# A blocked 8192 x 8192 transpose: four loads in two parts from two queues, no timing copies before a chunk, other places for the first stores

## The chip, the cores and the metric

The kernel runs on one core of a Trainium2 chip. The metric is the time of one execution on the device, in microseconds; lower is better. One more execution is taken with the profiler on, and every row below comes from that one.

## What is computed

```python
def setup_inputs():
    return {"x": np.random.randn(8192, 8192).astype(np.float32)}

def reference(x):
    return np.transpose(x)
```

The input has 268.4 MB and so has the output. Every element is read from HBM once and written once.

## The kernel before

**Tiles.** The input is cut into 128 chunks: chunk t holds 128 rows of x and 4096 columns, 2 MB. Chunks 0 to 63 cover the left half of the columns from top to bottom, 64 to 127 the right half. A chunk lies in SBUF with one row to a partition, 16 KB each. It is cut into 16 ranges of 256 columns. TensorE transposes a range as two 128 x 128 blocks (line 372, against the identity matrix `ident`), so a chunk takes 32 transposes, which fill two halves of PSUM: ranges 0 to 7 are evicted by ScalarE, 8 to 15 by VectorE (line 300, function `copies`).

**Stores.** A store collects up to 16 blocks of chunks that follow each other, so that long pieces go to HBM. Store w takes from chunk t the range with the index w modulo 16, for the 16 chunks t = w - 15 to w; the first fifteen stores are shorter, 1 to 15 cells, and after the last chunk fifteen shorter ones flush what is left. The range of chunk w that belongs to store w goes straight from PSUM to the store's region (the direct copy, "arena<-ps"); the ranges for later stores go to a buffer `slots` first, and the function `gather` (line 262, VectorE) moves what earlier chunks left there into the region, just before the direct copies of chunk w. In the program's order VectorE runs `gather(w)` and then `copies(w)`.

**Places in SBUF.** One buffer, `arena`, has 86 places of 1 KB in every partition. Three areas of 16 places hold loaded chunks; 38 further places are for the stores' regions (one of their areas holds an early chunk too, as four loads are under way at the start). A small planner (lines 114 to 153) walks over loads and stores in the order of their due times and gives each a place; `before` then names what has to have left that place: of a load, that its chunk is transposed, of a store, that it has landed. `gather` waits for these. From store 6 (`over`) on, a region starts at the lower or at the upper end of the 38 places, whichever comes free sooner, so from store 15 on two regions of 16 alternate.

**Order.** SP issues all transfers on one queue, in the order of the list `order`: store t - 1, then the load two to four chunks ahead of t. Before a store it waits for the direct copy (`closed`), before a load for the end of the transposes of the chunk in that area. Each transfer adds 16 to a semaphore, 1 for each of the 16 DMA engines that carry it.

**The start of a chunk.** For chunks 12 (`E`) to 125, TensorE waits for both halves of PSUM, runs two warming passes (line 366, `IDLE = 2`, 512 columns each, results overwritten), waits for `s_go`, then for the load's semaphore, and transposes. `s_go` comes from ScalarE: in the function `work`, it waits for the chunk's load and then runs `REST = 2` copies of the identity matrix into its half of PSUM, one after the other (line 405); what they write is overwritten by the transposes. They do nothing but take time. TensorE's part is a loop over three chunks (lines 387 to 391).

Of the kernel before, what the change touches and what calls it, by code (L numbers as in the profile page):

```python
# [40 lines left out]
def kernel(  # L41
# [5 lines left out]
    nc = tc.nc  # L47
    P = 128
    N, M = x.shape
    assert x.shape == out.shape[::-1]  # L50
    dt = x.dtype
# [10 lines left out]
    E = 12  # L62
# [48 lines left out]
    order += [("S", T - 1)] + [("S", w) for w in flush]  # L111


    due = {}
    sent = 0
    for k in order:
# [14 lines left out]
    for _, k, size, until in sorted(wanted):  # L131
        if k[0] == "L":
            o = spot(k[1])
        else:
            w = k[1]
            lo = NIN * NR if w < T - 2 else 0
            hi = END - NR if w < over else END
            late = lambda o: max([f for _, a, z, f in users if a < o + size and o < z], default=0)
            at = range(lo, hi - size + 1)
            if over <= w < T - 2:  # L140
                at = (lo, hi - size)
            elif w == T - 2:
                at = [spot(T - 3)]
            o = min(at, key=lambda o: (late(o), o))
        home[k] = o
        before[k] = sorted({u for u, a, z, _ in users if a < o + size and o < z}, key=lambda u: due[u])
        users = [
            (u, c, d, f)
            for u, a, z, f in users
            for c, d in ((a, min(z, o)), (max(a, o + size), z))  # L150
            if c < d
        ]
        users.append((k, o, o + size, until))

    with tc.tile_critical():  # L155
        ident = nc.alloc_sbuf_tensor("ident", [P, P], dt).ap()
        nc.alloc_sbuf_tensor("pad", [P, 64], dt)
        slots = nc.alloc_sbuf_tensor("slots", [P, (NR * (NR - 1) // 2) * PIECE], dt).ap()
        arena = nc.alloc_sbuf_tensor("arena", [P, END * PIECE], dt).ap()
        pss = [nc.alloc_psum_tensor(f"ps{k}", [P, J // 2], dt).ap() for k in range(2)]  # L160
# [5 lines left out]
        s_free = [nc.alloc_semaphore("s_fra"), nc.alloc_semaphore("s_frv")]  # L166
        s_cp = [nc.alloc_semaphore("s_cpa"), nc.alloc_semaphore("s_cpv")]
        s_g = nc.alloc_semaphore("s_g")
        s_go = nc.alloc_semaphore("s_go")
        s_rest = nc.alloc_semaphore("s_rest")  # L170
        s_x = [nc.alloc_semaphore("s_xa"), nc.alloc_semaphore("s_xv")]

        stored = [0] * (2 * W - 1)
# [4 lines left out]
        closed = {}  # L178
        shut = [0, 0]

        REST = 2
        LAST = T - 1 - (T - 1 - E) % NIN


# [11 lines left out]
        def free(eng, k):  # L198
            if k[0] == "L":
                eng.wait_ge(s_pe, 4 * k[1] + len(steps(k[1])))  # L200
            else:
                eng.wait_ge(s_st[lane(k[1])], done[k[1]])

        def load(t):
            s, c = divmod(t, CH)
            o = home["L", t] * PIECE
            for u in before["L", t]:
                free(nc.sync, u)
            nc.sync.dma_start(
                out=arena[:, o:o + J], in_=x[c * P:(c + 1) * P, s * J:(s + 1) * J]  # L210
            ).then_inc(s_ld[home["L", t]], 16)
# [126 lines left out]
        while order[first] == ("L", first) and not before[order[first]]:  # L338
# [11 lines left out]
            pattern=[[-1, P]],  # L350
            channel_multiplier=1,
        ).then_inc(s_id, 1)
        nc.scalar.sem_inc(s_free[0], 1)
        nc.vector.sem_inc(s_free[1], 1)

        def transposes(t):
            o = home["L", t]
            for g in range(NR):
                h, u = divmod(g, NR // 2)
                if u == 0 and not (h and E <= t < LAST):  # L360
                    nc.tensor.sem_inc(s_free[h], -1).wait_op(s_free[h], 1, "sem-ge")
                if g == 0:
                    if E <= t < LAST:
                        nc.tensor.sem_inc(s_free[1], -1).wait_op(s_free[1], 1, "sem-ge")  # L364
                        for _ in range(IDLE):
                            nc.tensor.matmul(out=pss[1][:, :4 * P], lhsT=ident, rhs=four, start=True, stop=True)  # L366
                    if E <= t < LAST:
                        nc.tensor.sem_inc(s_go, -1).wait_op(s_go, 1, "sem-ge")
                    nc.tensor.sem_inc(s_ld[o], -16).wait_op(s_ld[o], 16, "sem-ge")  # L369
                q = (o + range_at(t, g)) * PIECE  # L370
                for b in range(B):
                    tr = nc.tensor.transpose(  # L372
                        pss[h][:, (u * B + b) * P:(u * B + b + 1) * P],
                        arena[:, q + b:q + PIECE - B + b + 1:B],
                        ident,
                    )
                if g + 1 in steps(t):
                    tr.then_inc(s_pe, 1)
# [15 lines left out]
            transposes(t)  # L394

        worked = [0]
        rested = [0]

        def work(t):
            while worked[0] <= t:  # L400
                u = worked[0]
                if E <= u < LAST:
                    nc.scalar.wait_ge(s_ld[home["L", u]], 16)
                    for k in range(REST):
                        cp = nc.scalar.copy(  # L405
                            out=pss[0].rearrange("p (k i) -> p k i", i=P), in_=ap(ident, 0, [[0, J // 2 // P], [1, P]])
                        )
                        if k < REST - 1:
                            cp.then_inc(s_rest, 1)
                            rested[0] += 1  # L410
                            nc.scalar.wait_ge(s_rest, rested[0])
                    cp.then_inc(s_go, 1)
                gather(u, u)
                if u == T - 1:
                    gather(T, u)
                copies(u)
                worked[0] += 1
# [44 lines left out]
```

## Time and profile before

| What | Value |
|---|---|
| median of 3 runs | 1275.12 us |
| the runs | 1271.99, 1275.12, 1289.13 us |
| the profiled execution: its time | 1278.15 us |
| the profiled execution: its span | 1276.4 us |
| TensorE matmuls, share of the span | 66% |
| TensorE weight loads | 50% |
| VectorE | 48% |
| ScalarE | 54%, of it 426.3 us in 228 timing copies |
| DMA packets | 41334, 537.10 MB, mean 421 GB/s |

The span is what the profile covers; 1.75 us of the time lie outside it. PE is TensorE's matmuls, PEld its weight loads, DVE VectorE, ACT ScalarE, POOL GpSimd, SP the engine that issues the transfers; SPq or PEq is an engine's sequencer. "out<-in" names what is written and read; L28 is the line at which all stores but the first are issued, L209 that of the loads. "PEclk" is the granted TensorE clock, 1.00 being full speed, and "DMA share" the mean busy share of the 16 DMA engines; it can show a little over 1, as a packet is counted from before its predecessor's end. In a list of waits stand who waited and for whom, the total in us, how many times, and the longest. In a timeline stand the start, the length, and in brackets the idle time of the engine before it with what ended it.

### The profile page before, as it was taken

What the parts mean: (1) busy time and instruction counts of PE and PEld (TensorE: products, weight loads), DVE (VectorE), ACT (ScalarE), POOL (GpSimd) and SP (SyncE); (2) the same over time, 40 slices, a digit from 0 to 9 for tenths busy, and PEclk for the clock granted to TensorE, in tenths of its full rate; (3) what the DMA queues carried; (4) which work ended last, traced back from release to release, by engine and by line L of the source; (5) the groups of instructions that cost most, each with busy time, mean ns of one, the idle gap of its engine ahead of it and who ended that gap; (6) DMA issues with size and microseconds to landing.
All of it is one profiled execution on the core that took longest, in us unless ns stands there. A gap on an engine that the chain in (4) does not pass through costs nothing. (4 is left out here: it accounts for less than half of the span.)

```text
span 1276.4 us, 12056 instructions
## 1 busy us (share of the span) xinstructions
PE 837.0 (66%) x4552; PEld 642.4 (50%) x4552; DVE 615.1 (48%) x715; ACT 683.9 (54%) x630; POOL 0.7 (0%) x6
## 2 busy tenths in 40 slices
PE   6657866777676776666666666666666767666630
PEld 6655555544555555455545554554445545555530
DVE  3454454544554455445544544455445454455381
ACT  2235665566556556655665566555655556555510
POOL 0000000000000000000000000000000000000000
PEclk9877889988998889899898989999999898999865
DMA  9999999999999999999999999999999999999997
GB/s 394 412 413 361 412 428 430 428 432 430 432 430 432 430 432 430 432 430 432 429 428 430 429 429 430 431 431 432 431 431 432 430 399 420 426 428 419 407 396 327
DMA packets 41334, 537.10 MB, mean 421 GB/s; under 512 B 4576, under 2 KB 5216, under 8 KB 8288
## 3 DMA queue, kind: packets, MB, share of 16 engines
q1 hardware_dynamic: 41312, 536.89, 99.5%
q14 instruction: 18, 0.15, 0.0%
q8 instruction: 4, 0.07, 0.0%
HBM read 268.44 MB, written 268.44 MB: 421 GB/s over the span
## 5 line engine op out<-in xcount | busy, mean ns | idle before, releaser
L372 PEld LDWEIGHTS ps<-ident,arena 128*128 128x128 f32 x4096 | 553.6, 211 | 263.5 <-issue 263.5
L372 PE MATMUL ps<-ident,arena 128*128 128x128 f32 x4096 | 570.5, 303 | 156.7 <-PEq L369 156.2
L262 DVE COPY arena<-slots 128x2048 f32<-128x2048 f32 (+7 forms) x316 | 304.2, 1012 | 497.3 <-DMA out_dram<-arena 488.5
L405 ACT COPY ps<-ident 128x2048 f32<-128x2048 f32 x228 | 426.3, 1870 | 57.0 <-DMA arena<-in_x_dram 52.3
L366 PE MATMUL ps<-ident 128*128 128x512 f32 x456 | 270.4, 724 | 235.2 <-PEq L364 235.2
L300 ACT COPY slots<-ps 128x1024 f32<-128x1024 f32 (+2 forms) x335 | 238.5, 780 | 247.6 <-DVE arena L262 213.3
L300 DVE COPY slots<-ps 128x512 f32<-128x512 f32 (+2 forms) x336 | 289.4, 913 | 64.3 <-PE ps L372 62.8
L366 PEld LDWEIGHTS ps<-ident 128*128 128x128 f32 x456 | 88.8, 216 | 322.9 <-issue 322.9
L300 ACT COPY arena<-ps 128x256 f32<-128x256 f32 x66 | 24.5, 373 | 238.3 <-DVE arena L262 191.1
L300 DVE COPY arena<-ps 128x256 f32<-128x256 f32 x63 | 26.8, 425 | 77.4 <-PE ps L372 76.1
L300 ACT ACT_TABLE_LOAD x1 | 1.3, 1283 | 1.0 <-SPq L155 1.0
L344 POOL TENSOR_SCALAR_AFFINE_SELECT ident<-ident 128x128 f32<-128x128 f32 x1 | 0.3, 294 | 0.2 <-POOL ident L342 0.2
L342 POOL MEMSET ident<- 128x128 f32 x1 | 0.2, 205 | 0.5 <-SPq L155 0.5
L446 POOL MEMSET const-bfloat16-1.0<- 128x1 bf16 x1 | 0.1, 103 | 0.0
L446 POOL MEMSET const-uint8-127<- 128x1 uint8 x1 | 0.1, 103 | 0.0
L446 POOL MEMSET const-float32-0.0<- 128x1 f32 x1 | 0.1, 100 | 0.2 <-issue 0.2
L446 POOL MEMSET const-float32-1.0<- 128x1 f32 x1 | 0.1, 100 | 0.0
## 6 DMA issues: line engine op xcount, KB each, us to landing
arena<-in_x_dram SPq DMA_DIRECT2D x128, 2048.0 KB, 20.4
out_dram<-arena SPq DMA_DIRECT2D x98, 2048.0 KB, 16.6
out_dram<-arena SPq DMA_DIRECT2D x4, 1920.0 KB, 11.1
out_dram<-arena SPq DMA_DIRECT2D x4, 1792.0 KB, 11.1
out_dram<-arena SPq DMA_DIRECT2D x4, 1664.0 KB, 11.1
out_dram<-arena SPq DMA_DIRECT2D x4, 1536.0 KB, 10.8
out_dram<-arena SPq DMA_DIRECT2D x4, 1408.0 KB, 11.5
out_dram<-arena SPq DMA_DIRECT2D x4, 1280.0 KB, 12.4
```

Of the source, the lines that this page charges most:

```text
L262: cp = nc.vector.tensor_copy(out=ap(arena, do, [[P, len(v)], [dist, B], [1, P]]), in_=ap(slots, so, [[gap, len(v)], [P, B], [1, P]]),)
L300: cp = eng.copy(out=dst, in_=i) if e == 0 else eng.tensor_copy(out=dst, in_=i)
L342: nc.gpsimd.memset(ident, 0.0).then_inc(s_id, 1)
L344: nc.gpsimd.affine_select(out=ident, in_=ident, compare_op=mybir.AluOpType.not_equal, fill=1.0, base=0, pattern=[[-1, P]], channel_multipl ...
L366: nc.tensor.matmul(out=pss[1][:, :4 * P], lhsT=ident, rhs=four, start=True, stop=True)
L372: tr = nc.tensor.transpose(pss[h][:, (u * B + b) * P:(u * B + b + 1) * P], arena[:, q + b:q + PIECE - B + b + 1:B], ident,)
L405: cp = nc.scalar.copy(out=pss[0].rearrange("p (k i) -> p k i", i=P), in_=ap(ident, 0, [[0, J // 2 // P], [1, P]]))
L446: nc = _bacc.Bacc("TRN2", target_bir_lowering=False, num_devices=1)
```

## The change

**No timing copies.** `REST`, the copies of line 405 and the semaphores `s_go` and `s_rest` are gone. TensorE waits for the two halves of PSUM, runs the two warming passes, waits for the load and begins. ScalarE goes from the copies of one chunk straight to those of the next.

**Places of the first stores.** For stores 0 to 14 the list `young` names the place inside the 38, and the planner's choice is skipped. The places of stores 6 to 9 and 12 differ; all others keep theirs, but some of them follow other stores than before. So `gather` waits for other transfers:

| store | waited before for | waits now for |
|---|---|---|
| 7 | stores 0 to 3 | load 5 |
| 8 | load 5, store 6 | stores 0 to 3 |
| 9 | stores 3, 7 | stores 5, 6 |
| 10 | load 5, store 8 | load 5, stores 6, 7 |
| 11 | stores 4, 9 | stores 3, 4, 8 |
| 12 | load 5, store 10 | stores 4, 5, 9 |
| 14 | load 5, store 12 | stores 10, 12 |
| 15 | stores 4, 5, 13 | stores 12, 13 |
| 16 | load 5, store 14 | stores 12, 14 |

**Four loads in two parts.** Chunks 32, 60, 88 and 116 are loaded by `load_apart`: rows 0 to 119 by a DMA of GpSimd's, rows 120 to 127 by one of SP's at the place in SP's order where the whole load stood. Both queues wait first for the transposes of the chunk that was in the area. GpSimd waits for both landings and then adds 16 to the load's semaphore, for which TensorE waits as before. Ahead of the first of these loads, at the kernel's start, GpSimd copies 5 rows of 256 bytes into a spare buffer (`turn_engines(5)`), and ahead of each of the other three, right before it, 1 row (`turn_engines(1)`), and waits for that each time. The spare buffer has the size of the former `pad`. GpSimd's other work, making the identity matrix at the start, is as it was; otherwise it was idle.

```diff
+    young = [0, 1, 3, 6, 10, 15, 22, 29, 0, 17, 27, 0, 14, 0, 23]
...
-            if over <= w < T - 2:
+            if w < len(young):
+                at = [lo + young[w]]
+            elif w < T - 2:
                 at = (lo, hi - size)
...
-        nc.alloc_sbuf_tensor("pad", [P, 64], dt)
+        spare = nc.alloc_sbuf_tensor("spare", [P, 64], dt).ap()
...
-        REST = 2
...
+        APART = (32, 60, 88, 116)
+        PART = P - P // 16
+        gp = [0]
+
+        def turn_engines(n):
+            nc.gpsimd.dma_start(out=spare[:n, :], in_=x[:n, :64]).then_inc(s_gp, 16)
+            gp[0] += 16
+            nc.gpsimd.wait_ge(s_gp, gp[0])
+
+        def load_apart(t):
+            s, c = divmod(t, CH)
+            o = home["L", t] * PIECE
+            for u in before["L", t]:
+                free(nc.sync, u)
+                free(nc.gpsimd, u)
+            if t > APART[0]:
+                turn_engines(1)
+            nc.gpsimd.dma_start(
+                out=arena[:PART, o:o + J], in_=x[c * P:c * P + PART, s * J:(s + 1) * J]
+            ).then_inc(s_gp, 16)
+            nc.sync.dma_start(
+                out=arena[PART:, o:o + J], in_=x[c * P + PART:(c + 1) * P, s * J:(s + 1) * J]
+            ).then_inc(s_few, 16)
+            gp[0] += 16
+            nc.gpsimd.wait_ge(s_gp, gp[0])
+            nc.gpsimd.wait_ge(s_few, 16 * (APART.index(t) + 1))
+            nc.gpsimd.sem_inc(s_ld[home["L", t]], 16)
+
         def load(t):
             s, c = divmod(t, CH)
             o = home["L", t] * PIECE
+            if t in APART:
+                load_apart(t)
+                return
...
+        turn_engines(5)
...
-                    if E <= t < LAST:
-                        nc.tensor.sem_inc(s_go, -1).wait_op(s_go, 1, "sem-ge")
                     nc.tensor.sem_inc(s_ld[o], -16).wait_op(s_ld[o], 16, "sem-ge")
...
-                if E <= u < LAST:
-                    nc.scalar.wait_ge(s_ld[home["L", u]], 16)
-                    for k in range(REST):
-                        cp = nc.scalar.copy(
-                            out=pss[0].rearrange("p (k i) -> p k i", i=P), in_=ap(ident, 0, [[0, J // 2 // P], [1, P]])
-                        )
-                        if k < REST - 1:
-                            cp.then_inc(s_rest, 1)
-                            rested[0] += 1
-                            nc.scalar.wait_ge(s_rest, rested[0])
-                    cp.then_inc(s_go, 1)
                 gather(u, u)
```

More of the change, by code (lines that the diff above doesn't have):

```diff
@@ L168 @@
         s_g = nc.alloc_semaphore("s_g")
-        s_go = nc.alloc_semaphore("s_go")
-        s_rest = nc.alloc_semaphore("s_rest")
+        s_gp = nc.alloc_semaphore("s_gp")
+        s_few = nc.alloc_semaphore("s_few")
         s_x = [nc.alloc_semaphore("s_xa"), nc.alloc_semaphore("s_xv")]
@@ L396 @@
         worked = [0]
-        rested = [0]
         def work(t):
```

## The prediction

> **What bounds the kernel now.** I read the page first: what the DMA engines moved in each of 40 slices of the span, and how full the queues were.
>
> ```profile
> GB/s 394 412 413 361 412 428 430 428 432 430 432 430 432 430 432 430 432 430 432 429 428 430 429 429 430 431 431 432 431 431 432 430 399 420 426 428 419 407 396 327
> ...
> q1 hardware_dynamic: 41312, 536.89, 99.5%
> q14 instruction: 18, 0.15, 0.0%
> ```
>
> The packets of the data queue fill 99.5% of 16 DMA engines, at 430 to 432 GB/s through the middle: the kernel is bound by its transfers there. At 430 GB/s the 536.89 MB take 536,890 / 430 = 1248.6 us, so 27.8 us of the span of 1276.4 are lost somewhere. The busy time in ten stretches says where; it also shows TensorE busy for 546 of 800 us in the middle, and no other compute engine for more.
>
> ```profile
> core 0: us, PE busy (x) PEld busy (x) DVE busy (x) ACT busy (x) POOL busy (x), PEclk, DMA share, GB/s
> 0.00:20.00 20.00, 10.95 (x75) 10.82 (x76) 5.33 (x8) 5.42 (x8) 0.70 (x6) 1.00 0.92 377
> 20.00:100.00 80.00, 52.09 (x332) 48.68 (x331) 36.99 (x45) 24.78 (x35) 0.00 (x0) 0.81 1.01 415
> 100.00:130.00 30.00, 21.68 (x105) 16.10 (x104) 13.92 (x17) 16.51 (x14) 0.00 (x0) 0.81 0.90 355
> 130.00:200.00 70.00, 50.97 (x277) 37.85 (x276) 36.09 (x43) 43.40 (x43) 0.00 (x0) 0.90 1.00 421
> 200.00:1000.00 800.00, 546.04 (x2951) 411.18 (x2949) 392.30 (x454) 468.04 (x418) 0.00 (x0) 0.92 1.01 430
> 1000.00:1210.00 210.00, 142.38 (x738) 105.47 (x738) 99.58 (x114) 119.57 (x105) 0.00 (x0) 0.90 1.00 418
> 1210.00:1232.00 22.00, 12.94 (x85) 12.26 (x83) 15.92 (x20) 6.13 (x10) 0.00 (x0) 0.81 0.91 385
> 1232.00:1269.40 37.40, 0.00 (x0) 0.00 (x0) 14.99 (x19) 0.00 (x0) 0.00 (x0) 0.50 1.00 415
> 1269.40:1274.20 4.80, 0.00 (x0) 0.00 (x0) 0.00 (x0) 0.00 (x0) 0.00 (x0) 0.50 0.07 27
> 1274.20:1276.40 2.20, 0.00 (x0) 0.00 (x0) 0.00 (x0) 0.00 (x0) 0.00 (x0) 0.50 0.00 0
> ```
>
> A stretch loses its length times (1 - rate / 430): 2.5 us to 20, 2.8 to 100, 5.2 to 130, 1.5 to 200, nothing from there to 1000, 5.9 to 1210, 2.3 to 1232, 1.3 to 1269.4, 4.5 to 1274.2 and 2.2 to the end, together 28.2. Two kinds are to be told apart. Where the DMA share is about 1.01, the engines always had packets and these were slow (20 to 100, 130 to 200, 1000 to 1210). Where it is lower, engines had nothing to do: 100 to 130 (0.90), 1210 to 1232 (0.91) and the last row but one. There the share is 0.07, about one engine of 16 (0.0625), and the rate is 27 GB/s, a sixteenth of 430: for 4.8 us a single DMA engine works off what the other fifteen have long finished. It is that much behind.
>
> Next the waits, and a stretch of the timeline in the steady part.
>
> ```profile
> DVE arena L262 <- DMA out_dram<-arena: 488.5, 114, 11.5
> ```
> ```profile
> 1130.15 0.54 SPq L28 DMA_DIRECT2D out_dram<-arena  x1
> ...
> 1132.16 3.77 ACT L405 COPY ps<-ident 128x2048 f32<-128x2048 f32 x2 [0.35 <-DMA arena<-in_x_dram]
> ...
> 1132.38 1.95 PE L366 MATMUL ps<-ident 128*128 128x512 f32 x4 [1.88 <-PEq L364]
> ...
> 1136.22 4.08 PE L372 MATMUL ps<-ident,arena 128*128 128x128 f32 x32 [1.89 <-PEq L369]
> 1137.10 2.43 DVE L262 COPY arena<-slots 128x2048 f32<-128x2048 f32 x3 [4.92 <-DMA out_dram<-arena]
> ...
> 1139.96 0.55 SPq L28 DMA_DIRECT2D out_dram<-arena  x1
> ```
>
> One chunk takes 1139.96 - 1130.15 = 9.8 us from store to store. The load lands at 1132.2, the timing copies hold TensorE to 1136.2, but the store's issue hangs on another chain: VectorE waits 4.92 us for an earlier store to leave the region, copies for 2.43, and 0.4 us after that the store is issued. That wait comes 114 times, 488.5 us in all. So in the middle nothing but the DMA engines sets the pace, and a chunk that is transposed sooner waits for the region all the same.
>
> **The change part by part.** *No timing copies.* Gone are 228 copies on ScalarE and TensorE's wait for them. The two warming passes of line 366 stay, and they begin only at 1132.38, when VectorE has freed its half: without the copies the transposes start at 1132.38 + 1.95 = 1134.3 in place of 1136.2, 1.9 us sooner. What hides this gain is the region wait: the gather ends at 1139.5, the transposes at 1140.3 now and 1138.4 then. For the few chunks whose direct copy comes last, the store is issued up to 0.8 us sooner, into a queue that isn't empty. I take 0. Fewer instructions to fetch could give back a part of q14's 0.15 MB, 5.6 us on one engine at 27 GB/s if all were on one; I take 0 of it too, and bound the whole part by 0 and -1.9 us, one chunk's lead.
>
> *Regions of the first stores.* The gathers of chunks 8 and 11 wait for stores issued just before them:
>
> ```profile
> 64.56 1.23 DVE L262 COPY arena<-slots 128x2048 f32<-128x2048 f32 x1 [11.51 <-DMA out_dram<-arena]
> ...
> 88.47 1.82 DVE L262 COPY arena<-slots 128x768 f32<-128x768 f32 x2 [4.89 <-DMA out_dram<-arena]
> ```
> ```profile
> 90.78 0.54 SPq L28 DMA_DIRECT2D out_dram<-arena  x1
> 91.36 0.59 SPq L209 DMA_DIRECT2D arena<-in_x_dram  x1
> 103.07 0.54 SPq L28 DMA_DIRECT2D out_dram<-arena  x1
> 103.65 0.59 SPq L209 DMA_DIRECT2D arena<-in_x_dram  x1
> 114.44 0.54 SPq L28 DMA_DIRECT2D out_dram<-arena  x1
> 115.03 0.59 SPq L209 DMA_DIRECT2D arena<-in_x_dram  x1
> 123.02 0.54 SPq L28 DMA_DIRECT2D out_dram<-arena  x1
> ```
>
> By the planner's own account, region 8 now follows stores 0 to 3 and no longer load 5 and store 6, and region 11 follows stores 3, 4 and 8 and no longer 4 and 9. The 11.51 us and 4.89 us largely go, the queue stays deeper, and the 12 us holes between the issues at 90.78, 103.07 and 114.44 meet a queue with work in it. The engines' idle time there is 30 x (1.01 - 0.90) = 3.3 us; that is the most it can give, and 0 the least. I take -3: both waits stand right before the hole, and nothing later does. What is late next is TensorE's own cycle in the same stretch (103.07 to 114.44, then 123.02), which the timing copies no longer lengthen.
>
> *Four loads apart.* A row is 16 KB, at 27 GB/s 0.61 us of one engine. [...] The other 8 rows go by SP: 1 row on each of eight engines, or at worst 8 rows on one. [...] The waits: GpSimd waits for the slot, the tiny copy, both landings, and has nothing else queued; SP issues the 8 rows at the load's old place and goes on to the next store. TensorE waits for GpSimd's word. Cover for this is the time from issue to landing:
>
> ```profile
> arena<-in_x_dram SPq DMA_DIRECT2D x128, 2048.0 KB, 20.4
> out_dram<-arena SPq DMA_DIRECT2D x98, 2048.0 KB, 16.6
> ```
>
> A load now takes 20.4 us, nearly all of it behind others, 2 MB being 4.9 us at 430 GB/s. GpSimd's packets stand in no such line if the engines serve two queues in turn, and then land in about 2 x 4.9 = 9.8 us plus the tiny copy. How the engines share two full queues no row shows; the price of mixing lies between 0 and the slowdown of the first slices: 361 in place of 430 GB/s over four stretches of 9.8 us is 39 x 0.19 = 7.5 us. I take 0, by the middle, where loads and stores mix at full rate.
>
> The sum: 1278.15 (the profiled execution, 1.75 us above its span) - 3 - 3 = 1272.2. The median of the runs shown, 1275.12, is 3.0 below that execution, so 1269 us.
>
> **The rivals.**
>
> [...] Chance 0.22.
>
> *TensorE's clock falls and TensorE becomes the bound* (the other side). Now the copies split TensorE's work into 1.95 and 4.08 us with pauses of 1.9; afterwards it is one piece of 6.0 and a pause of 3.8. The clock is 0.50 where TensorE rests (1232 on) and 0.92 in the middle. In the stretch 100 to 130, at 0.81, stores went out every (123.02 - 90.78) / 3 = 10.7 us. If the longer pause keeps it there, each of the 114 chunks costs 10.7 - 9.8 = 0.9 us more: +103, about 1370. It decides once the cycle from VectorE's freeing to the next passes 9.8 us. Against it: that stretch had the timing copies and the region waits in its cycle as well, and 1.95 + 4.08 = 6.0 us fill 9.8 only at a mean clock under 0.92 x 6.0 / 9.8 = 0.57. [...] Chance 0.06.
>
> *GpSimd's loads come late or mix badly.* If the tiny copy has to wait out a line as the stores do (16.6 us) and the load another (20.4), TensorE gets the chunk 37 us after the slot is free, not 20.4. Without it the engines still have 20.4 - 4.9 us of the line and two more chunks, 2 x 9.8: 35 us; the way from landing to store takes 1139.96 - 1132.16 = 7.8 of them. From about 28 us on each us is lost, so 9 us for each of the three loads with a tiny copy: 1275.1 + 27 - 6 = 1296. With two queues served in turn and only the mixing price, 1275.1 + 7.5 - 6 = 1277. With both it is 1296 + 7.5 = 1304, past 2%. Chance 0.14, of which 0.04 past 2%.
>
> **How the numbers follow.** Forecast 0.58, rivals 0.22, 0.06 and 0.14. Likeliest 1269 us. All that the first stores, the lone engine and the idle 2.2 us of 1210 to 1232 could give is 3.3 + 4.8 + 2.2 = 10.3, or 1265, and the runs' own scatter (1271.99 to 1289.13) reaches 3 us below the median: low 1262. The high end takes in the second case and most of the third: 1284. 2% is about what this measurement can tell from no change: 25.5 us, below 1249.6 or above 1300.6. Faster than that would need 25.5 of the 28 us that are lost against the steady rate: 0.01. Slower: 0.06 + 0.04 = 0.10. Within: 0.89.
>
> **What would show it.** Right: a DMA share near 1.0 between 100 and 130 us; no stretch of several us with share 0.07 at the end; VectorE's waits for stores before 90 us shorter; transposes about 2 us after the landing, and 200 to 1000 us still at 430 GB/s. Wrong: a rate below 430 around the four loads, TensorE waiting for GpSimd's word, a clock well under 0.9 with store-to-store times over 9.8 us, or a lone engine at the end as before.

## The result, and the profile after

| | median | runs | ratio to before, 95% interval |
|---|---|---|---|
| before, runs beside the changed kernel | 1276.90 us | 1271.99 to 1289.13 (4) | |
| changed kernel | 1295.39 us | 1291.70 to 1297.34 (4) | 1.0130 [1.0088, 1.0173] |

The changed kernel is 1.3% slower, 18.5 us by the medians. The forecast was 1269 us in a range of 1262 to 1284. Ratios here and below leave disturbed runs out, which the medians do not, so a ratio is not exactly the quotient of the medians beside it. The profiled execution after took 1291.7 us, its span is 1289.9.

First the page after: the rate in 40 slices of 32.2 us, the queues, and from its list of DMA issues the loads of the two queues (KB each, median us from issue to landing).

```profile
GB/s 393 415 426 430 430 429 429 429 328 429 431 430 432 430 431 431 430 365 411 423 422 429 428 430 432 408 417 430 431 431 431 430 431 406 352 392 430 432 403 335
...
q1 hardware_dynamic: 40800, 529.02, 97.3%
q0 software_dynamic: 704, 7.87, 2.2%
...
arena<-in_x_dram SPq DMA_DIRECT2D x124, 2048.0 KB, 20.8
...
arena<-in_x_dram POOLq DMA_DIRECT2D x4, 1920.0 KB, 18.3
...
spare<-in_x_dram POOLq DMA_DIRECT2D x3, 0.2 KB, 5.8
```

The hole of the fourth and fifth slices (361 and 412 before) is gone. Four new ones stand in its place: 328 in the ninth slice, 365 in the 18th, 408 in the 26th, 352 in the 35th. GpSimd's queue, q0, is in the list now: it moved 7.87 of 536.89 MB, 1.5% of the bytes, and its packets fill 2.2 of 99.5 parts of the engines' time, 2.2%. So a byte of it costs 1.5 times a byte of the rest. Its four loads did not come late: 18.3 us from issue to landing, against 20.8 for SP's; with the tiny copy of 5.8 us that goes ahead of three of them it is 24.1 us, still less than the 28 us from which the prediction counted a loss.

The busy time in stretches cut at the four holes (us of each engine, the granted clock, DMA share, GB/s):

```profile
core 0: us, PE busy (x) PEld busy (x) DVE busy (x) ACT busy (x) POOL busy (x), PEclk, DMA share, GB/s
20.00:100.00 80.00, 57.17 (x382) 52.97 (x381) 40.02 (x49) 21.96 (x34) 0.00 (x0) 0.89 1.01 421
100.00:130.00 30.00, 20.40 (x93) 13.59 (x94) 15.55 (x19) 6.77 (x11) 0.00 (x0) 0.83 1.01 430
...
258.00:282.00 24.00, 13.52 (x50) 8.64 (x51) 5.75 (x8) 2.40 (x4) 0.00 (x0) 0.71 1.00 300
282.00:545.00 263.00, 191.37 (x967) 143.91 (x966) 129.54 (x148) 54.05 (x86) 0.78 (x2) 0.84 1.01 430
545.00:567.00 22.00, 11.08 (x67) 8.34 (x65) 7.25 (x9) 2.06 (x4) 0.25 (x1) 0.88 0.99 366
567.00:829.00 262.00, 190.32 (x972) 143.90 (x972) 129.55 (x156) 54.11 (x85) 1.52 (x2) 0.85 1.00 423
829.00:848.00 19.00, 7.99 (x37) 5.69 (x38) 7.34 (x8) 4.04 (x7) 0.00 (x0) 0.74 1.00 373
848.00:1106.00 258.00, 187.75 (x952) 141.34 (x951) 124.72 (x143) 51.81 (x79) 1.02 (x2) 0.85 1.01 428
1106.00:1133.00 27.00, 14.21 (x60) 10.85 (x60) 10.67 (x12) 4.04 (x7) 0.00 (x0) 0.72 0.88 313
...
1283.30:1287.20 3.90, 0.00 (x0) 0.00 (x0) 0.00 (x0) 0.00 (x0) 0.00 (x0) 0.50 0.06 26
```

With the prediction's rule, length times (1 - rate / 430), the four holes lose 24 x (1 - 300/430) = 7.3, 3.3, 2.5 and 7.3 us, together 20.4. In the first three the DMA share is 0.99 or 1.00: the engines are full the whole time, and what they carry is slow. That is not what a late load looks like. In the fourth the share is 0.88: there, engines also had nothing to do for a part of it. The stretch 567 to 829 loses another 4.3 us. Won are 5.2 us from 100 to 130 (355 GB/s before, 430 now) and 1.1 us from 20 to 100. The lone engine at the end is still there: 3.9 us at share 0.06, where it was 4.8.

Two views show the first stores and the steady part. VectorE's timeline has the gathers of chunks 8 and 11, which waited 11.51 and 4.89 us before:

```profile
53.44 1.23 DVE L297 COPY arena<-slots 128x2048 f32<-128x2048 f32 x1 [0.41 <-DVE slots L335]
...
79.57 1.82 DVE L297 COPY arena<-slots 128x768 f32<-128x768 f32 x2 [3.54 <-DMA out_dram<-arena]
```

And a stretch of the timeline of all engines in the steady part:

```profile
342.68 0.55 SPq L28 DMA_DIRECT2D out_dram<-arena  x1
...
344.90 1.96 PE L402 MATMUL ps<-ident 128*128 128x512 f32 x4 [2.51 <-PEq L400]
...
346.70 3.99 PE L406 MATMUL ps<-ident,arena 128*128 128x128 f32 x32
...
349.70 2.43 DVE L297 COPY arena<-slots 128x2048 f32<-128x2048 f32 x3 [5.00 <-DMA out_dram<-arena]
...
352.56 0.54 SPq L28 DMA_DIRECT2D out_dram<-arena  x1
...
354.78 3.75 PE L402 MATMUL ps<-ident 128*128 128x512 f32 x4 [4.10 <-PEq L400]
```

The load landed at 344.66, the transposes start 2.0 us later (4.06 before), VectorE's wait for the region is 5.00 us (4.92 before), and from store to store it is 352.56 - 342.68 = 9.9 us. The 2 us that this chunk's transposes gain are hidden by the wait for the region, as forecast. Not every chunk runs like this one: the warming passes of the next take 3.75 us in place of 1.96, at a granted clock of 0.50 in place of 1.00. That too is hidden, as long as a chunk takes 9.9 us: this one's store is issued at 362.28, 9.7 us after the one before.

### The profile page after: what moved, and what is told of

The parts are those of the page before. It is cut to its first block, busy times and chain, and to the rows that moved or that the text cites. A ratio compares the mean times of both kernels' runs of the same rounds, so it can differ in the third digit from the quotient of the medians.

```text
span 1289.9 us, 11726 instructions
## 1 busy us (share of the span) xinstructions
PE 874.1 (68%) x4552; PEld 671.7 (52%) x4552; DVE 614.7 (48%) x715; ACT 257.4 (20%) x402; POOL 5.9 (0%) x14
## 3 DMA queue, kind: packets, MB, share of 16 engines
q0 software_dynamic: 704, 7.87, 2.2%
## 5 line engine op out<-in xcount | busy, mean ns | idle before, releaser
L406 PEld LDWEIGHTS ps<-ident,arena 128*128 128x128 f32 x4096 | 571.8, 212 | 145.4 <-issue 145.4
L406 PE MATMUL ps<-ident,arena 128*128 128x128 f32 x4096 | 571.9, 304 | 42.2 <-PEq L403 42.2
L402 PE MATMUL ps<-ident 128*128 128x512 f32 x456 | 322.9, 848 | 325.9 <-PEq L400 325.9
L402 PEld LDWEIGHTS ps<-ident 128*128 128x128 f32 x456 | 99.9, 242 | 424.9 <-issue 424.9
L225 POOL DMA_DIRECT2D arena<-in_x_dram x4 | 3.1, 764 | 269.7 <-PE ps L406 253.0
## 6 DMA issues: line engine op xcount, KB each, us to landing
arena<-in_x_dram SPq DMA_DIRECT2D x124, 2048.0 KB, 20.8
arena<-in_x_dram POOLq DMA_DIRECT2D x4, 1920.0 KB, 18.3
out_dram<-arena SPq DMA_DIRECT2D x4, 1664.0 KB, 14.4
```

The source lines that it names most:

```text
L225: nc.gpsimd.dma_start(out=arena[:PART, o:o + J], in_=x[c * P:c * P + PART, s * J:(s + 1) * J]).then_inc(s_gp, 16)
L406: tr = nc.tensor.transpose(pss[h][:, (u * B + b) * P:(u * B + b + 1) * P], arena[:, q + b:q + PIECE - B + b + 1:B], ident,)
```

## The experiments

A name with `a_` is an edit of the changed kernel, one with `b_` of the kernel before.

### The three parts, each alone

`a_noapart` is the changed kernel with the four loads whole and on SP's queue again.

```diff
-        APART = (32, 60, 88, 116)
+        APART = ()
...
-        turn_engines(5)
```

> The changed kernel with all 128 loads whole on SP's queue (no GpSimd load, no tiny copies); the new places of the first stores and the missing timing copies stay. Theory M (two full queues on the same DMA engines slow every packet while both are busy): the four dips of the changed kernel (328, 365, 408 and 352 GB/s in slices of 32 us, together some 28 us) go, so 1262 to 1268 us, below the kernel before. Theory C (the lost timing copies lower the clock, 0.84 for 0.89, and make chunks late): still 1288 to 1297. Theory I (only the uneven shares cost, up to 0.61 us for each row more on an engine): 1286 to 1291, as the four loads then give back 2.4 us on seven engines and no more.

Measured: 1287.35 us (1281.49 to 1290.56), 1.0076 [1.0032, 1.0120]. That is just below the range of theory C and far from that of theory M. So the split loads are not the whole of it: without them, a kernel that has the new places and lacks the timing copies is still behind the kernel before.

`b_apart` is the kernel before with the split loads and nothing else.

```diff
+        APART = (32, 60, 88, 116)
...
+        def load_apart(t):
...
+        turn_engines(5)
```

> The kernel before with the four loads in two parts alone (timing copies and places as before). Theory M: four dips as in the changed kernel, 28 us less up to 4.8 for the lone engine: 1297 to 1305 us. Theory C: no slower than before, 1270 to 1278. Theory I: up to 2.4 us either way, 1273 to 1280.

Measured: 1298.89 us (1294.21 to 1300.63), 1.0166 [1.0125, 1.0207]: the split alone costs 20 us by the medians, as much as the whole change.

`b_young` is the kernel before with the places of the first stores and nothing else; `b_young2` is the same kernel with more runs, as the first interval reached past 1.

```diff
+    young = [0, 1, 3, 6, 10, 15, 22, 29, 0, 17, 27, 0, 14, 0, 23]
...
-            if over <= w < T - 2:
+            if w < len(young):
+                at = [lo + young[w]]
+            elif w < T - 2:
```

> The kernel before with the new places of the first stores alone. All theories: the DMA share between 100 and 130 us rises from 0.90 to 1.0, worth up to 3.3 us of idle time: 1271 to 1275 us. If the places are worth nothing: 1275 to 1278.

> The kernel before with the new places of the first stores alone, once more with more rounds. Theory S: the idle time of 100 to 130 us is gone (5 us), but the engines then enter the middle some 3 us apart instead of meeting at 120 us, come 9 us apart about 100 us sooner and lose more late: no gain in the whole, 1274 to 1284 us, with a wider scatter than before. If the places give what they give at the start: 1270 to 1273.

Measured: 1281.66 us (1265.31 to 1293.23), 0.9955 [0.9883, 1.0028] at first; then 1271.16 us (1265.39 to 1280.57, 12 runs), 0.9935 [0.9911, 0.9959]. The places are worth 7 us by the medians, and this kernel is faster than both. Theory S, which saw no gain in the whole, was wrong here.

`b_norest` is the kernel before without the timing copies.

```diff
-                    if E <= t < LAST:
-                        nc.tensor.sem_inc(s_go, -1).wait_op(s_go, 1, "sem-ge")
...
-                if E <= u < LAST:
-                    nc.scalar.wait_ge(s_ld[home["L", u]], 16)
-                    for k in range(REST):
...
-                    cp.then_inc(s_go, 1)
```

> The kernel before without the timing copies alone. Theory S: the copies carry no time; the holes of 100 to 130 us stay and still set the drift back: 1270 to 1280 us, landings of one load within 1 us at 120 us. Theory C: 1283 to 1292 as a_noapart, with a clock of 0.83 to 0.84.

Measured: 1290.65 us, with a wide scatter (1273.02 to 1335.04), 1.0061 [1.0013, 1.0108]. By the ratio, taking the copies out costs 8 us here; the median lies in the range of theory C. On top of the places it costs more: `a_noapart` is `b_young2` without them, 1287.35 against 1271.16, or 16 us. Whether the clock is the reason, as theory C has it, is taken up below.

### What is slow in a split load

Three things come together in it: a second queue, GpSimd as the issuer, and a division into 120 and 8 rows. `a_sp_both` keeps the division and has both parts issued by SP, on one queue.

```diff
-                free(nc.gpsimd, u)
-            if t > APART[0]:
-                turn_engines(1)
-            nc.gpsimd.dma_start(
+            nc.sync.dma_start(
                 out=arena[:PART, o:o + J], in_=x[c * P:c * P + PART, s * J:(s + 1) * J]
```

> The changed kernel with the 120 rows issued by SP too, right ahead of its 8 rows: the same split in two parts and the same word from GpSimd to TensorE, but one queue. Theory M: no dips, within 5 us of a_noapart, 1262 to 1272. If the split itself or GpSimd's word costs (theory I): dips or waits at the four loads stay, above 1280. Where the lone engine at the end is now also tells which it is: if it is the engine that gets no share of the 120 rows on this queue, it is no longer last.

Measured: 1359.36 us (1344.21 to 1376.31), 1.0558 [1.0491, 1.0624], much slower. Its profiled execution is the slowest of its runs, so its lines are read for their direction more than for their size:

```profile
core 0: us, PE busy (x) PEld busy (x) DVE busy (x) ACT busy (x) POOL busy (x), PEclk, DMA share, GB/s
264.00:288.00 24.00, 17.33 (x93) 12.63 (x91) 12.04 (x15) 4.85 (x8) 0.00 (x0) 0.86 1.01 406
...
600.00:1000.00 400.00, 266.82 (x1270) 194.35 (x1268) 172.56 (x204) 72.00 (x114) 0.00 (x0) 0.80 0.96 373
```

Around the first such load (264 to 288 us) 24 x (1 - 406/430) = 1.3 us are lost, where the changed kernel lost 7.3. So a second queue is not needed for a loss at such a load, but on one queue it is smaller there. Most of this kernel's time goes later, from 600 us on, with the first and the last of a transfer's 16 completions 12 to 15 us apart; the next section comes back to that distance. It goes from 3.6 to 7.0 us across the first of these loads. By its packets the 120 rows leave one engine out on SP's queue too: 41340, 28 more than in `before`, fit 15 and 8 completions in place of 16, four times. If that engine had been the late one, the distance should have shrunk.

`a_gp_whole` keeps queue and issuer, and takes the division away: all 128 rows by GpSimd, no part by SP, no tiny copies.

```diff
-            nc.gpsimd.dma_start(
-                out=arena[:PART, o:o + J], in_=x[c * P:c * P + PART, s * J:(s + 1) * J]
+            nc.gpsimd.dma_start(
+                out=arena[:, o:o + J], in_=x[c * P:(c + 1) * P, s * J:(s + 1) * J]
             ).then_inc(s_gp, 16)
-            nc.sync.dma_start(
...
-            nc.gpsimd.wait_ge(s_few, 16 * (APART.index(t) + 1))
```

> As a_noapart, but the four loads go whole, 128 rows, on GpSimd's queue, with no part on SP and no tiny copies. Theories M and G: dips as in the changed kernel, about 7 us each, 1285 to 1300. Theory I (the split in 120 and 8 rows costs): no dips, as a_noapart.

Measured: 1273.34 us (1270.93 to 1275.51), 0.9963 [0.9928, 0.9998]. Its DMA issues, and its stretches at the four loads:

```profile
arena<-in_x_dram POOLq DMA_DIRECT2D x4, 2048.0 KB, 14.4
```
```profile
core 0: us, PE busy (x) PEld busy (x) DVE busy (x) ACT busy (x) POOL busy (x), PEclk, DMA share, GB/s
258.00:282.00 24.00, 16.02 (x72) 11.63 (x72) 9.86 (x13) 3.64 (x6) 0.15 (x1) 0.79 1.01 432
...
530.00:552.00 22.00, 11.98 (x53) 7.83 (x52) 8.65 (x12) 3.98 (x6) 0.86 (x1) 0.77 1.01 426
552.00:810.00 258.00, 188.59 (x960) 141.93 (x959) 128.12 (x153) 52.89 (x83) 0.33 (x1) 0.85 1.01 424
810.00:829.00 19.00, 10.04 (x44) 6.79 (x45) 6.51 (x9) 3.35 (x7) 0.19 (x1) 0.77 1.01 431
...
1088.00:1115.00 27.00, 16.22 (x72) 11.55 (x72) 12.04 (x16) 5.76 (x11) 0.00 (x0) 0.75 0.90 365
```

Where the changed kernel has 300, 366 and 373 GB/s, this one has 432, 426 and 431. The fourth place is slow in both: of the 7.3 us that the changed kernel loses there, this one loses 27 x (1 - 365/430) = 4.1 as well, and the share of 0.90 says that engines had nothing to do. Packet by packet, the first load of each kernel (16 KB packets while GpSimd's are under way; counted from the trace):

```
                        GpSimd's packets     SP's packets    both queues
120 + 8 rows   after    mean 1065 ns         mean 989 ns     213 to 328 GB/s, 17 us long
128 rows  a_gp_whole    mean  611 ns         mean 611 ns     418 to 451 GB/s,  8 us long
```

While two queues of 128-row transfers share the engines, nothing is lost; behind such a load the rate is lower for a while (424 GB/s from 552 to 810 us, where `a_noapart` has 430). With the division, SP's packets are nearly as slow as GpSimd's, though they belong to ordinary transfers of 128 rows. The first of the four loads has no tiny copy right before it and has the same hole.

`a_act` puts the same four loads, whole, on ScalarE's queue.

```diff
+            if t in (32, 60, 88, 116):
+                for u in before["L", t]:
+                    free(nc.scalar, u)
+                nc.scalar.dma_start(
+                    out=arena[:, o:o + J], in_=x[c * P:(c + 1) * P, s * J:(s + 1) * J]
+                ).then_inc(s_ld[home["L", t]], 16)
+                return
```

> As a_noapart, but loads 32, 60, 88 and 116 go whole, 128 rows, on ScalarE's queue, a second queue of the same kind as SP's. Theory M (two full queues on one DMA engine cost, whoever made them): dips at the four loads as with GpSimd's, slices of 32 us at 330 to 410 GB/s, about 7 us each. Theory G (only GpSimd's queue is slow): no dip below 425 at 250 and 550 us. The total time is disturbed by the late part either way: 1270 to 1310.

Measured: 1272.83 us (1270.26 to 1277.38), 0.9973 [0.9939, 1.0007]. Again no hole while these loads are under way (at the second, 430 GB/s from 540 to 560 us; right behind it 390 GB/s to 580 us, 1.9 us lost), and a gain of 14 us over `a_noapart`, from which it differs in nothing but the queue of four loads.

`a_halves` stays on SP's queue and divides evenly: chunks 32 and 88 into two times 64 rows, 60 and 116 into two halves of the columns, each with all 128 rows.

```diff
+                    if t in (32, 88):
+                        r, k = slice(h * P // 2, (h + 1) * P // 2), slice(0, J)
+                    else:
+                        r, k = slice(0, P), slice(h * J // 2, (h + 1) * J // 2)
+                    nc.sync.dma_start(
```

> As a_noapart, one queue, but four loads are cut in two even DMAs: loads 32 and 88 by rows (twice 64 rows of 16 KB), loads 60 and 116 by columns (twice 128 rows of 8 KB). Every engine has the same bytes in all of them. Theory P (what is slow is a load whose rows are dealt to the engines otherwise than the 128 rows of all other loads): dips below 400 GB/s over some 10 us at about 270 and 830 us, none at about 550 us (at 1110 us the late part disturbs). Theory U (uneven shares are what is slow): no dip at any of the four. Time 1285 to 1300 with P, 1281 to 1291 with U.

Measured in a single run: 1300.81 us. Its stretches, the second with chunk 32, the third with chunk 60, the last with chunk 88:

```profile
core 0: us, PE busy (x) PEld busy (x) DVE busy (x) ACT busy (x) POOL busy (x), PEclk, DMA share, GB/s
240.00:264.00 24.00, 18.48 (x83) 13.07 (x83) 9.61 (x11) 3.92 (x5) 0.00 (x0) 0.80 1.01 429
264.00:288.00 24.00, 18.22 (x99) 14.22 (x97) 10.14 (x12) 3.98 (x6) 0.00 (x0) 0.85 1.01 354
...
540.00:564.00 24.00, 19.34 (x104) 14.72 (x103) 11.74 (x13) 3.98 (x6) 0.00 (x0) 0.84 1.00 429
...
816.00:840.00 24.00, 15.48 (x76) 11.62 (x75) 9.57 (x10) 4.04 (x7) 0.00 (x0) 0.79 1.01 347
```

Halves of the rows are slow, 24 x (1 - 354/430) = 4.2 us for one load and 4.6 for the other, though 64 rows divide evenly among 16 engines (the queue has 41632 packets, 320 more than in `a_noapart`: 256 for the halved rows and 16 completions for each of the four transfers more). In both holes the share is 1.01, and from 271 to 280 us a packet of 16 KB takes 1187 ns in the median, where 611 is usual. Halves of the columns are not slow. So neither a second queue, nor two transfers in place of one, nor an uneven share is needed; what the slow ones have in common is that a transfer does not span all 128 rows. That the same makes the load of 120 and 8 rows slow is concluded from this, and not why it loses 7.3 us on two queues and 1.3 on one: that stays open.

The sizes fit each other. An estimate from the packets of `a_halves`: at 1187 ns in place of 611 the stretch from 271 to 280 us loses 9 x (1 - 611/1187) = 4.4 us, and by the rate it is 4.2. With the division in 120 and 8 rows the packets of both queues are slow, 1065 ns on GpSimd's and 989 on SP's. Why fewer rows make packets slow, no run here shows.

### What the timing copies held up

With the split loads out of the way, 16 us remain to be explained between `b_young2` and `a_noapart`. The stretches of `a_noapart`:

```profile
core 0: us, PE busy (x) PEld busy (x) DVE busy (x) ACT busy (x) POOL busy (x), PEclk, DMA share, GB/s
100.00:130.00 30.00, 20.69 (x97) 14.14 (x97) 15.32 (x18) 7.09 (x12) 0.00 (x0) 0.83 1.00 428
...
600.00:900.00 300.00, 215.36 (x1085) 161.51 (x1086) 145.22 (x173) 60.36 (x95) 0.00 (x0) 0.84 1.01 430
...
1000.00:1100.00 100.00, 70.97 (x341) 49.62 (x341) 48.02 (x56) 19.96 (x31) 0.00 (x0) 0.83 1.00 416
1100.00:1210.00 110.00, 74.91 (x361) 54.91 (x360) 48.04 (x54) 19.90 (x30) 0.00 (x0) 0.81 0.97 382
1210.00:1240.00 30.00, 18.48 (x98) 17.23 (x96) 16.96 (x20) 6.13 (x10) 0.00 (x0) 0.72 0.74 303
```

Full rate to 900 us, and then a decline. The first stores' hole is gone, so the loss is late. A DMA's 16 completion increments give a clue (672 for the 42 loads of one area in `before`; in the profile after, 15 come late for 120 rows and 8 for 8 rows, so they are read as one for each engine): the time between the first and the last of them says how far the engines have drifted apart.

```
mean us between the first and the last completion of a DMA, and GB/s
from      before       a_noapart    a_drain      b_young2     a_act
 200 us   3.6  430     3.5  431     3.5  429     3.6  430     2.8  429
 500      4.7  431     5.3  431     5.8  431     5.2  431     4.4  422
 800      6.8  431     7.8  432     1.9  421     7.0  429     5.5  420
 900      8.0  430     8.6  425     3.6  429     7.6  425     5.7  431
1000      8.5  418    10.0  416     3.8  431     9.1  412     6.4  431
1100      9.0  420    12.7  386     3.8  431    10.6  402     5.9  418
```

(Each row is 100 us. From 600 to 800 us stores go out in two parts that share a semaphore, so these rows are left out.)

In the three kernels of the table that nothing interrupts, `before`, `a_noapart` and `b_young2`, the distance grows, and the rate falls once it is about 8 us (7.6 to 8.6 in the table). The theory: SP issues a store and a load every 9.8 us, which is as much work as an engine does in that time (4.19 MB at 430 GB/s are 9.8 us); the last engine always has a backlog, but the first ones live on what the distance leaves of it, and when that is used up they run dry between two issues. `a_noapart` shows the signs from 1100 us on: a share of 0.97 and then 0.74, and 16.2% of SP's 16 KB packets longer than 640 ns, where it is 0.1 to 0.3% in the middle. But from 1000 to 1100 us its engines are still full (1.00) at 416 GB/s, and in `before` they are at 418: what is lost there is lost in slow packets, and why a large distance goes with slow packets is open.

`a_drain` tests it: SP waits once, before load 70, until a store issued shortly before has landed, so that all engines come to the same point.

```diff
+            if t in (70,):
+                nc.sync.wait_ge(s_st[lane(t - 3)], done[t - 3])
```

> The changed kernel without the four GpSimd loads (as a_noapart), and with one wait added: before it issues load 70, SP waits until store 67, issued just before, has landed, so all DMA engines run empty once, at about 650 us. Theory S (the engines drift apart; once the last is some 9 us behind the first, the first run dry between two issues, and each joint restart slows packets of the last one too; an empty queue sets the drift back): the rate from 1000 us to the last load stays at 425 to 431 GB/s in place of 398, the wait costs about 3 us, 1260 to 1268 us, faster than without the wait and than the kernel before. Theory C (the lost timing copies): no gain late, the wait adds 3 to 17 us to 1287: 1288 to 1304.

Measured: 1275.25 us (1273.43 to 1277.15), 0.9976 [0.9946, 1.0006]. One wait added, 12 us won over `a_noapart`. The time is outside the ranges of both theories. Its stretches:

```profile
core 0: us, PE busy (x) PEld busy (x) DVE busy (x) ACT busy (x) POOL busy (x), PEclk, DMA share, GB/s
640.00:680.00 40.00, 25.99 (x117) 18.04 (x118) 15.23 (x18) 6.62 (x12) 0.00 (x0) 0.79 0.86 320
...
1000.00:1100.00 100.00, 73.21 (x381) 54.10 (x380) 49.60 (x57) 19.84 (x29) 0.00 (x0) 0.86 1.01 431
1100.00:1210.00 110.00, 78.40 (x404) 58.52 (x402) 55.86 (x65) 23.95 (x37) 0.00 (x0) 0.86 1.01 431
```

The wait costs 40 x (1 - 320/430) = 10.2 us there and some more in the slices behind it, the distance goes from 6.5 us for one load to 0.8 for the next, and the end runs at 431 GB/s, where `a_noapart` has 416 and 382. So the gain that theory S named came, but the wait cost over three times the 3 us that it allowed. Theory C falls: the mean clock is 0.838, where `a_noapart` has 0.835. `a_act` gets the like for less. Its loads on the second queue are themselves only 0.6 to 1.0 us apart, and the distance of the transfers around them goes from 6.6 to 4.4 us across the one near 820 us and from 7.1 to 4.7 across the one near 1100, though not across the one near 545 (4.5 and 4.7). From 1000 to 1100 us it has 431 GB/s.

Two more kernels ask whether more of that helps: `a_act_more` has eight loads on ScalarE's queue, `a_act_all` all from chunk 15 on (the edits against `a_act`).

```diff
-            if t in (32, 60, 88, 116):
+            if t in (24, 36, 48, 60, 72, 84, 96, 108):
```
```diff
-            if t in (32, 60, 88, 116):
+            if t >= 15:
```

> As a_act, but eight loads (24, 36, and so on to 108) go whole on ScalarE's queue. Theory S (a load on a second queue lets the engines meet again before they are 9 us apart): the distance between first and last landing stays under 7 us, the rate from 1000 us on at 425 to 430 GB/s; each of the eight costs 1 to 3 us: 1266 to 1274 us. If the four of a_act helped for another reason (fewer loads in SP's line): another 4 us less than a_act, 1264 to 1270.

> As a_act, but all loads from 15 on go on ScalarE's queue, so that SP's has the stores alone. Theory S: two queues are free of cost (611 ns a packet); stores land sooner, as no load stands before them, so the queue of stores is shorter and the engines run dry earlier: 1270 to 1290 us. If two queues simply balance the engines: 1262 to 1268.

Measured: 1275.26 us, 0.9956 [0.9930, 0.9982], and 1275.59 us, 0.9985 [0.9962, 1.0008]. No further gain: four are enough. The first is just above the range of theory S, the second inside it.

Last, whether the copies matter where the drift is held down in another way. `b_young_act` is `b_young2` with the four loads of `a_act`, so it is `a_act` with the timing copies; `b_act` is the kernel before with those four loads and its old places. Both differ from what they start from in the same lines:

```diff
+            if t in (32, 60, 88, 116):
+                for u in before["L", t]:
+                    free(nc.scalar, u)
+                nc.scalar.dma_start(
...
+                return
```

> The kernel before with the new places of the first stores and with loads 32, 60, 88 and 116 whole on ScalarE's queue; the timing copies stay. Theory S: within 3 us of a_act (1272.8): the timing copies carry no time. Theory C: 8 us or more below a_act, 1258 to 1265.

> The kernel before with loads 32, 60, 88 and 116 whole on ScalarE's queue alone; places and timing copies as before. With b_young_act beside it this gives the worth of the new places where the late loss is held down: 3 to 5 us slower than b_young_act if they give there what they give at the start, 1277 to 1281; the same time if not.

Measured: `b_young_act` 1276.14 us (1271.62 to 1281.59), 0.9974 [0.9950, 0.9997]; `b_act` 1281.75 us (1277.66 to 1288.06), 1.0023 [0.9999, 1.0047]. With and without the copies it is 0.9974 and 0.9973: beside four whole loads on a second queue they are worth nothing, and 16 us without these loads. It is not the TensorE clock: the two have mean clocks of 0.874 and 0.839 and the same time. That the loads hold the drift down in both is not shown: the profile of `b_young_act`, of its longest run, has distances of 8.6 us and 412 GB/s from 1000 to 1100 us. The places are worth 5.6 us in this pair. But four loads on the second queue do not add to `b_young2`, which stays the best at 0.9935. Each of them costs some rate behind it (422 and 420 GB/s in two rows of the table for `a_act`, 430 to 432 in `a_noapart`); that `b_young2` has too little to win back is a guess, as its own profile falls to 412 and 402 GB/s, in an execution 6.6 us above its median.

From the kernel before to the changed one there is a chain of kernels, by medians: places -7, copies gone +16, four loads on a second queue -14, their division +22 (1295.39 against 1273.34 of `a_gp_whole`). Whatever its steps, such a chain adds up to the whole difference, so its sum proves nothing, and the worth of a step depends on what else is in the kernel: the copies cost 8, 16 or nothing. In the changed kernel the division is the step that decides. The split alone (+20) and the places alone (-7) make +13 of the 18.5 us. The 5 that remain for the copies are an estimate, as a kernel with the split, the places and the copies was not run; by the ratios it is 1.0166 x 0.9935 = 1.010 against 1.013, and the intervals overlap.

## Why the prediction was wrong

**The price of the division.** This step failed. The prediction took 0 for "mixing", with 7.5 us in all as the worst, from the first slices of the kernel before, where one queue of 128-row transfers is slow for another reason (in the slice at 361 GB/s engines were idle, share 0.90). It measured 20 us alone (`b_apart`), and 22 against the same loads whole. The prediction looked for the price in the two queues, and these mix for nothing (611 ns a packet in `a_gp_whole`). As far as the runs show, the price lies in rows: halves of 64 rows are slow and halves of the columns are not, and a transfer that spans 120 rows slows its own packets to a mean of 832 to 1065 ns and the other queue's with them; the four holes lose 20.4 us, of which 4.1 in the fourth stand in `a_gp_whole` too. No row of the profile before shows a transfer of 2 MB over fewer than 128 rows, and the prediction treated the number of rows as a question of shares alone.

**The relief of the late engine.** The second -3 of the sum, and half of the 6 in the rivals' sums, stand for it: the four loads were to spare one and the same engine, the late one. No run shows this term; what the runs showed in its place is a lone engine at the end of 3.9 us, against 4.8. In the profile after, one of the 16 completions of each of GpSimd's parts of 120 rows came 6.4 to 10.2 us before the other fifteen, which is read as one engine without rows each time. That it was the same one each time is not shown: of the tiny copies the one of 5 rows went as 5 packets of 256 bytes, but each of the three of 1 row as 16 packets of 16 bytes. Which engine is late, and whether it was a spared one, stays open for GpSimd's transfers; on SP's queue `a_sp_both` speaks against it.

**The timing copies.** Taken as 0, bounded by -1.9. For the kernel before and for the one with the new places this is wrong as well, and on the other side of the bound: +8 and +16. In the changed kernel itself some 5 us remain for it, not clear of the noise. The cover named, the region wait, is there (5.00 us), and the chunk's cycle is the same. What was missed is that the loss from 1000 to 1210 us, read correctly as "the engines always had packets and these were slow", goes with a distance that builds up over the whole run: at 800 us it is 7.0 with the copies (`b_young2`) and 7.8 without (`a_noapart`), at 1100 us 10.6 and 12.7. That the copies slow the drift is not shown by this: the profile of `b_young`, the same kernel as `b_young2` in an execution of 1293.23 us, has 7.2 and 13.1. What the copies do is open; no run varied their number or length.

**The places of the first stores.** Right in direction and place, too small: -3 (0 to -3.3) was taken from the idle engines between 100 and 130 us, and 5.2 us came back there, since packets in that hole were slow too, with 1.1 us from 20 to 100. By the medians it is 7. So this term was mis-sized: a hole costs its lost rate, not its idle share alone.

**The rivals.** "GpSimd's loads come late or mix badly" named the right place and the wrong reason: the loads did not come late (24.1 us with the tiny copy, not 37), and that its 1296 us is close to what was measured is luck, as it is made of lateness that did not occur. The rival at 0.22, that the late engine is another than the one a split load leaves out, is borne out as far as the end shows, and is a detail beside the 20 us. The clock rival fell: the mean clock did go down, from 0.891 to 0.837, but the cycle is 9.9 us. A line of the page before and one of the page after have the warming passes, with the mean of one in ns:

```profile
L366 PE MATMUL ps<-ident 128*128 128x512 f32 x456 | 270.4, 724 | 235.2 <-PEq L364 235.2
```
```profile
L402 PE MATMUL ps<-ident 128*128 128x512 f32 x456 | 322.9, 848 | 325.9 <-PEq L400 325.9
```

The mean pass takes 848 ns in place of 724. It is not so at each chunk: after the pause of 4.10 us before 354.78 the four take 3.75 us, at a granted clock of 0.50, but after 2.51 us, before 344.90, they take 1.96, at 1.00. From store to store these two chunks take 9.7 us with the slow four and 9.9 with the fast.

**The signs** named beforehand came out so: the share near 1 from 100 to 130, the shorter waits and the earlier transposes as for "right"; the rate below 430 around the four loads, a clock well under 0.9 with 9.9 us from store to store, and the lone engine as for "wrong". TensorE's waits before the transposes are 42.2 us in all, against 37.6 in `a_noapart`, so it hardly waited for GpSimd's word. The sign on the four loads was the one that decided.

## What to carry to other kernels

Where the DMA engines are the bound, a transfer's price is not in its bytes alone: here one that leaves out 8 of 128 rows slowed everything beside it (300 GB/s in place of 430 at the first load), and a whole transfer on a second queue was the cheaper way to relieve or to reorder (1273.34 us on GpSimd's, against 1295.39). Before a copy or a wait that "does nothing" is taken out, look whether the rate falls towards the end of the run, and measure how far a transfer's 16 completions lie apart early and late (3.5 us and 12.7 in `a_noapart`); one wait at the right place may pay for itself (in `a_drain` it cost 10.2 us, and the kernel was 12 us faster than `a_noapart`). And when a change has several parts, try each alone: here a part worth 7 us was buried under one that costs 20, and a third part cost 16 us or nothing, depending on what stood beside it.

## What the runs showed of the hardware that was not expected

- Transfers of 128 rows on two queues shared the engines without loss while both were under way, 611 ns a packet on each in `a_gp_whole`; behind such a load the rate was lower for a while (390 GB/s from 560 to 580 us in `a_act`). GpSimd's loads in `a_gp_whole` landed in 14.4 us, sooner than SP's (20.7), and the first one's packets went on at 611 ns beside a copy of VectorE's within SBUF (266.51 to 268.86 us).
- Transfers of 120 rows, or of 64, slowed all packets under way: 1065 and 989 ns on the two queues at the first load of the changed kernel, 300 GB/s; 354 and 347 GB/s for 64 and 64 rows in `a_halves`, a single run, and 429 there for halves of the columns.
- The 16 engines drifted apart under a full queue: 3.5 us at 200 us, 7.8 at 800, 12.7 at 1100 in `a_noapart`, and one wait of SP's brought them from 6.5 back to 0.8 in `a_drain`. Why some engines are slower than others over the run no run here tells.
